# Accumulator banks of the third chunk pair, order of evacuations, and place of the first parted hidden chunks in a two-layer transformer kernel

## The chip, the cores and the metric

The kernel runs on one core of a Trainium2 chip. The metric is the device time of one execution in microseconds; the time before is the median of 3 runs. The engines are TensorE (PE, with its weight loads PEld), VectorE (DVE), ScalarE (ACT), GpSimd (POOL) and SyncE (SP, which here issues the loads of the weights).

## The reference

Two layers (DEPTH = 2), a sequence of 512 tokens, model width 1024, hidden width 2816. In each layer two feed-forward stages stand around a mix of three attention branches:

```python
def _swiglu(x, w1, w2):
    gt, up = jnp.split(x @ w1, 2, axis=-1)
    return (jax.nn.silu(gt) * up) @ w2

for l in range(DEPTH):
    x = _layer_norm(DN_ALPHA * x + 0.5 * _swiglu(x, ffn1_w1[l], ffn1_w2[l]), ln1_g[l], ln1_b[l])
    mix = _token_mix(x, w_in[l], ...)
    x = _layer_norm(DN_ALPHA * x + mix, ln2_g[l], ln2_b[l])
    x = _layer_norm(DN_ALPHA * x + 0.5 * _swiglu(x, ffn2_w1[l], ffn2_w2[l]), ln3_g[l], ln3_b[l])
```

The change lies in the feed-forward stages, of which there are four: FFN1 and FFN2 of layer 0, FFN1 and FFN2 of layer 1.

## The kernel before

**Parts.** Every fp32 operand is held as a high part and a low part (`hi`/`lo` for weights, `xh`/`xl` for the activations), and a product is three matmuls: hi·hi, hi·lo, lo·hi. ACT makes a high part by a rounding copy, DVE the low part by a subtraction (L159 and L160 in `wsplit`). The parts of weights lie in rotating buffers of several pools; `unit()` deals them out in a fixed cycle. In the feed-forward stage the cycle over seven units is: shared pool `wt` (3 buffers), `more` twice, `w1` twice, `wt` twice.

**Stages of a feed-forward block** (`ffn`). The hidden width is cut into 22 chunks of 128. For chunk `f` a gate and an up column block are multiplied with the activations, and `evac` writes Silu(gate)·up to the hidden buffer (L380 on ACT, then L381 on DVE).

1. Chunks 0 and 1 are done in `staged`: four accumulators `pj` (gate 0, up 0, gate 1, up 1), all with the first 256 tokens, then all with the second 256. Their weights were prepared during the stage before. Between the first products the transposes of the last token blocks of the normalised activations run (`second`, L238; L240 and L241 take them out of PSUM), two banks for token block 2 and two for token block 3.
2. Chunk 2 is a plain pair, `pg` and `pu`, each 24 matmuls of 512 columns (L180 to L182).
3. Chunks 3 to 21 compute gate and up together with seven half-size products in place of eight (`seven` prepares the weights, `seven_products` multiplies). `seven` loads two raw blocks through SP (L304, L306), splits the gate block (`ug`, L159 and L160), forms two sums and differences on DVE (`x1`, `x2`, L312 to L315), parts them (`u1`, `u2`, L317 and L318) and parts half of the up block (`ud`: `dh`, `dl`, L319 and L320). The order of the products is `ug`, `u1`, `u1`, `u2`, `ud`, `ug`, `u2`: 12 half-size matmuls each (L334), 84 in a chunk. They use three accumulators, `pg`, `pu`, `pv`. The activations' side needs sums over tokens (`token_sums`, L362 to L367), made once for each stage; `lth` is their last ACT and last DVE instruction.
4. `rows_ln` multiplies the hidden chunks with the rows of the second weight matrix into eight accumulators `acc` (L193 to L195) and applies the layer norm. A hidden chunk is parted before (`h_parts`, L386 and L387); chunks 0 and 1 are parted into one `hi` and one `lo` buffer of the shared pool `wt`, before the loop's last chunk is prepared (L417 to L420), the others into buffers of their own.

**PSUM banks.** There are eight, under four tags: `mm` 2, `sc` 3, `tp` 2, `po` 1. `ps()` without a tag deals them out in a ring: the counter `ring[0]` picks the tag, and each tag rotates its own buffers. Four accumulators `pj` and four transposes make eight, so the ninth and tenth allocations, `pg` and `pu` of chunk 2, come back to the ring places of the first `pj` pair.

**Order.** PE and POOL follow the order in which the program is written. ACT, DVE and SP are ordered by a scheduler when the program is built; `behind(a, b)` tells it to issue what follows no earlier than instructions a and b. Before the change, chunks 3, 4 and 5 and the evacuations of chunks 0, 1 and 2 are all behind `lth`. In the order built from that, ACT takes after chunk 3's first split the Silu table load, the two Silus of chunks 0 and 1 and chunk 4's split, and then both L317 of chunk 3; DVE does the two L381 and chunk 4's L160 before chunk 3's L318. At the end, ACT and DVE part hidden chunks 0 and 1 before they split chunk 21's weights.

Of the kernel before, what the change touches and what calls it, by code (L numbers as in the profile page):

```python
# [10 lines left out]
F32 = mybir.dt.float32  # L11
F32R = mybir.dt.float32r
BF = mybir.dt.bfloat16
AF = mybir.ActivationFunctionType
OP = mybir.AluOpType
# [4 lines left out]
P = 128  # L20
S, D, F = 512, 1024, 2816
KD, KF, NB = D // P, F // P, S // P
# [43 lines left out]
def body(tc, a, out, depth=DEPTH):  # L66
    nc = tc.nc
# [7 lines left out]
    wt = pool("wt")  # L75
# [4 lines left out]
    ring = [0]  # L80
# [50 lines left out]
    lnq = K()  # L131
    lnq.sq = None

    def behind(*ins):

        st = ExitStack()
        for i in ins:
            if i:
                st.enter_context(tc.issue_after(i))
        return st  # L140
# [150 lines left out]
    PLAIN = (0, 1, 2)  # L291
# [6 lines left out]
    def seven(w, ca, cb, pl, ru):  # L298

        v = w.rearrange("(k p) f -> p k f", p=P)
        rg = wraw()
        nc.sync.dma_start(rg, v[:, :, ca:ca + P])  # L304
        ru = ru or wraw()
        nc.sync.dma_start(ru, v[:, :, cb:cb + P])  # L306
        ug, u1, u2 = wsplit(rg), unit(), unit()
        ud = [pl.tile([P, 4, P], F32R, name=n, tag=n) for n in ("dh", "dl")]
        h1, h2 = slice(0, 4), slice(4, 8)
        x1, x2 = [pl.tile([P, KD, P], F32, name="ws", tag="ws", bufs=2) for _ in range(2)]  # L310
        tt = nc.vector.tensor_tensor
        tt(x1[:, h1], ru[:, h1], ru[:, h2], op=OP.add)  # L312
        tt(x1[:, h2], x1[:, h1], rg[:, h1], op=OP.subtract)
        tt(x2[:, h1], rg[:, h1], ru[:, h1], op=OP.subtract)
        tt(x2[:, h2], rg[:, h2], x1[:, h2], op=OP.subtract)  # L315
        for (hi, lo), x in ((u1, x1), (u2, x2)):
            nc.scalar.activation(hi, x, AF.Copy)  # L317
            tt(lo, x, hi.bitcast(F32), op=OP.subtract)  # L318
        nc.scalar.activation(ud[0], ru[:, h2], AF.Copy)  # L319
        tt(ud[1], ru[:, h2], ud[0].bitcast(F32), op=OP.subtract)  # L320
        return ug, u1, u2, ud

    def seven_products(ws, t, pl, u, nb):

        (ug, u1, u2, ud), (t1, t2, t3, t4) = ws, t
        ga, pa, pb = ps(name="pg"), ps(name="pu"), ps(name="pv")
        p_, r_, s_ = [(xh[:, k:k + 4, c], xl[:, k:k + 4, c]) for k, c in ((0, H1), (4, H1), (4, H2))]

        def prod(o, w, k0, x, first=True):
            for k in range(4):  # L330
                hi, lo = w[0][:, k0 + k], w[1][:, k0 + k]
                vh, vl = x[0][:, k], x[1][:, k]
                for i, (wx, vx) in enumerate(((hi, vh), (hi, vl), (lo, vh))):
                    nc.tensor.matmul(o, wx, vx, start=first and k == 0 and i == 0, stop=k == 3 and i == 2,  # L334
                                     skip_group_check=True)

        tt = nc.vector.tensor_tensor
        prod(ga[:, H1], ug, 0, p_)
        prod(ga[:, H2], u1, 0, t1, False)
        sn = pl.tile([P, S], F32, name="sn", tag="sn", bufs=nb)  # L340
        nc.scalar.activation(sn, ga, AF.Copy)  # L341
        prod(pa[:, H1], u1, 4, t2)
        prod(pa[:, H2], u2, 0, t3, False)
        v = pl.tile([P, S], F32, name="v", tag="v", bufs=nb)
        tt(v[:, H1], pa[:, H1], sn[:, H1], op=OP.add)
        tt(v[:, H2], pa[:, H2], v[:, H1], op=OP.add)
        prod(pb[:, H1], ud, 0, t4)
        tt(u[:, H1], pb[:, H1], v[:, H2], op=OP.add)
        tt(u[:, H2], sn[:, H2], v[:, H2], op=OP.add)
        prod(ga[:, H1], ug, 4, r_, False)  # L350
        prod(ga[:, H2], u2, 4, s_, False)
        tt(ga[:, H2], ga[:, H2], v[:, H1], op=OP.add)
        return ga
# [15 lines left out]
    def ffn(l, w1, w2, which, xap, xa, wts, pend, done_prev, last, nxt, late=None):  # L369


        st = K()
        NA = KF - NTAIL

        def hpart(f):
            return (st.ha, st.hb)[f >= NA][:, f - NA * (f >= NA)]

        def evac(f, pg, pu):
            t = st.lnp.tile([P, S], F32, name="t", tag="t", bufs=2)
            nc.scalar.activation(t, pg, AF.Silu)  # L380
            nc.vector.tensor_tensor(hpart(f), t, pu, op=OP.mult)  # L381

        hs = {}

        def h_parts(k, t):
            nc.scalar.activation(t[:, 0], hpart(k), AF.Copy)  # L386
            nc.vector.tensor_tensor(t[:, 1], hpart(k), t[:, 0].bitcast(F32), op=OP.subtract)  # L387
            hs[k] = t

        pts = staged(wts, pend)  # L390
        for tb in range(NB):
            nc.gpsimd.dma_start(x_sp[tb * P:(tb + 1) * P, :], xa[tb])
        done_prev()
        xap.release()
        st.w1p = nx.w1 = pool("w1p", side="right", reuse_waits="tile")
        more.n = 4
        with behind(lnq.sq):
            wp = [(wcols(w1, f * P), wcols(w1, F + f * P)) for f in PLAIN[2:]]

        for n, shape, dt, nb in (("hi", [P, KD, P], F32R, 2), ("lo", [P, KD, P], F32R, 2), ("dh", [P, 4, P], F32R, 1),  # L400
                                 ("dl", [P, 4, P], F32R, 1), ("raw", [P, KD, P], F32, 1), ("sn", [P, S], F32, 2),
                                 ("v", [P, S], F32, 2), ("ws", [P, KD, P], F32, 2)):
            st.w1p.tile(shape, dt, name=n, tag=n, bufs=nb)
        th, tl = (st.w1p.tile([P, 4, 4, 256], F32R, name=n) for n in ("th", "tl"))
        tpl, nb = (pre_t, 6) if late else (st.w1p, 2)
        lth = [token_sums(k, lambda: tpl.tile([P, KD, P], F32, name="ws", tag="ws", bufs=nb)
                          .rearrange("p a s -> p (a s)"), th, tl) for k in range(4)][-1]
        st.t = [(th[:, i], tl[:, i]) for i in range(4)]
        if late:
            late()  # L410
        fb = pool("fb", reuse_waits="tile")
        st.lnp = pool("lnp", reuse_waits="tile")
        fa = pool("fa", reuse_waits="tile")
        st.hb = fb.tile([P, NTAIL, S], F32, name="hb")
        st.ha = fa.tile([P, NA, S], F32, name="ha")
        for f in range(2, KF):
            if f == KF - 1:  # L417
                for k, n in enumerate(("hi", "lo")):
                    h_parts(k, wt.tile([P, KD, P], F32R, name=n, tag=n, bufs=3)
                            .rearrange("p (a b) c -> p a (b c)", a=2))  # L420
            if f not in PLAIN:
                ru = nx.w1.tile([P, KD, P], F32, name="raw", tag="raw") if f % 2 else None
                with behind(*(lth if f < 6 else ())):
                    ws = seven(w1, f * P, F + f * P, nx.w1, ru)
                    if f == PLAIN[-1] + 1:
                        evac(0, pts[0], pts[1])
                        evac(1, pts[2], pts[3])
                        for x in wp:
                            evac(*x)
                evac(f, seven_products(ws, st.t, nx.w1, hpart(f), 2), hpart(f))  # L430
                continue
            wg, wu = wp.pop(0)
            pg, pu = ps(name="pg"), ps(name="pu")
            proj(pg, wg)
            proj(pu, wu)
            wp.append((f, pg, pu))
        nx.w1 = None
        st.w1p.tile([P, 88], F32, name="pad")
        st.w1p.release()
        xap, xa = alloc_xa()  # L440
        for tb in range(NB):
            nc.gpsimd.dma_start(xa[tb], x_sp[tb * P:(tb + 1) * P, :])
        hsp = pool("hsp", side="right", reuse_waits="tile")
        ln = LN(hsp, which, l, xa, 0.5, last)

        def wload(k):
            if k not in hs:
                h_parts(k, hsp.tile([P, 2, S], F32R, name="hs", tag="hs", bufs=6))
            w = wrows(w2, k)
            if after and k > 2:  # L450
                i, h = after.pop(0)
                nc.gpsimd.tensor_copy(pace, w[1][:, 0, 0:1].bitcast(F32))
                nc.gpsimd.dma_start(bvec[i, h:h + 1], bsml[i, h:h + 1, None, :].to_broadcast([1, P, TLEN]))
            return w

        wts, pend = rows_ln(KF, wload, lambda k: hs[k][:, 0], lambda k: hs[k][:, 1], ln, NA, fa.release, nxt)

        def done():
            nx_close()
            hsp.release()  # L460
            st.lnp.release()
            fb.release()

        return wts, pend, done, xap, xa
# [983 lines left out]
```

## Time and profile before

| | |
|---|---|
| Median of 3 runs | 2504.3 us (2503.48 to 2506.77) |
| The profiled execution, own time | 2505.77 us |
| Its span | 2504.0 us |
| Mean granted TensorE clock | 0.993 |
| DMA | 286.29 MB, mean 114 GB/s |
| ACT L159 waits for raw weight loads, total | 62.7 us in 26 waits |
| Loads of feed-forward weights | 264, 512 KB each, 3.9 us to landing |

A row of a timeline has start, duration, engine, line, operation, output and inputs, and in brackets the idle time of the engine before it with what ended it. A row of the waits has who waited for whom, the total, the number of times and the longest. A row of windows has the busy time of each engine in a stretch of the span, then the granted clock and the DMA share. The chunk numbers in the text are the loop index `f`. Chunk 2 begins at 41.0 us (FFN1, layer 0), 927.3 (FFN2, layer 0), 1281.2 (FFN1, layer 1) and 2166.4 (FFN2, layer 1).

### The profile page before, as it was taken

What the parts mean: (1) busy time and instruction counts of PE and PEld (TensorE: products, weight loads), DVE (VectorE), ACT (ScalarE), POOL (GpSimd) and SP (SyncE); (2) the same over time, 40 slices, a digit from 0 to 9 for tenths busy, and PEclk for the clock granted to TensorE, in tenths of its full rate; (3) what the DMA queues carried; (4) which work ended last, traced back from release to release, by engine and by line L of the source; (5) the groups of instructions that cost most, each with busy time, mean ns of one, the idle gap of its engine ahead of it and who ended that gap; (6) DMA issues with size and microseconds to landing.
All of it is one profiled execution on the core that took longest, in us unless ns stands there. A gap on an engine that the chain in (4) does not pass through costs nothing.

```text
span 2504.0 us, 42423 instructions
## 1 busy us (share of the span) xinstructions
PE 2465.6 (98%) x16411; PEld 2213.7 (88%) x16411; DVE 1795.1 (72%) x3661; ACT 1173.1 (47%) x2208; POOL 228.7 (9%) x454
## 2 busy tenths in 40 slices
PE   9999999999999989999999999999999999899998
PEld 8999887788889889998899998878888998899986
DVE  7997355587688688974499963566777886888734
ACT  4544334477644444543344443345666444444431
POOL 2000210133300000000000000002332000000000
PEclk9999999999999999999999999999999999999999
DMA  6333543633134433334334343445322344333341
GB/s 189 114 106 100 194 118 119 179 81 93 44 101 136 140 102 97 109 93 160 101 105 115 102 145 109 133 116 149 101 74 68 93 135 135 95 108 102 109 144 59
DMA packets 378106, 286.29 MB, mean 114 GB/s; under 512 B 17464, under 2 KB 349384, under 8 KB 377904
## 3 DMA queue, kind: packets, MB, share of 16 engines
q1 hardware_dynamic: 370496, 258.68, 35.1%
q0 software_dynamic: 7408, 24.90, 2.8%
q8 instruction: 129, 2.11, 0.3%
q14 instruction: 73, 0.60, 0.1%
HBM read 256.22 MB, written 17.88 MB: 109 GB/s over the span
## 4 chain that ended last, share of the span: by engine, by line
PE 93%; DVE 4%; DMA 1%; ACT 1%; issue 1%; SPq 0%; DVEq 0%; POOLq 0%; ACTq 0%; POOL 0%
PE pg L334 21%; PE pu L334 10%; PE acc L194 8%; PE acc L193 8%; PE acc L195 8%; PE pv L334 5%; PE pj L180 5%; PE pj L181 4%; PE pj L182 4%; PE brp L180 2%; PE brp L181 2%; PE brp L182 2%; PE sN L913 2%; PE ptN L955 1%; PE po L974 1%; PE sF L834 1%
## 5 line engine op out<-in xcount | busy, mean ns | idle before, releaser
L160 DVE TENSOR_TENSOR lo<-raw,hi 128x1024 fp32r<-128x1024 f32 (+1 forms) x314 | 375.9, 1203 | 310.4 <-ACT hi L159 303.9
L159 ACT ACTIVATE hi<-raw 128x1024 fp32r<-128x1024 f32 (+1 forms) x314 | 324.4, 1040 | 416.0 <-PE acc L194 195.8
L334 PE MATMUL pg<-xh,hi 128*128 128x256 f32 x1104 | 312.4, 283 | 0.2 <-ACT sn L341 0.2
L334 PE MATMUL pg<-xh,lo 128*128 128x256 f32 x1104 | 312.4, 283 | 0.0
L334 PE MATMUL pg<-xl,hi 128*128 128x256 f32 x1104 | 312.4, 283 | 0.0
L317 ACT ACTIVATE hi<-ws 128x1024 fp32r<-128x1024 f32 x184 | 193.8, 1058 | 169.5 <-DVE ws L315 47.3
L180 PE MATMUL pj<-xh,hi 128*128 128x512 f32 (+1 forms) x720 | 267.6, 372 | 0.6 <-ACT hi L159 0.6
L318 DVE TENSOR_TENSOR lo<-ws,hi 128x1024 fp32r<-128x1024 f32 x184 | 224.1, 1221 | 57.7 <-ACT hi L317 57.4
L182 PE MATMUL pj<-xh,lo 128*128 128x512 f32 (+1 forms) x720 | 255.2, 354 | 0.0
L181 PE MATMUL pj<-xl,hi 128*128 128x512 f32 (+1 forms) x720 | 254.9, 354 | 0.1
L193 PE MATMUL acc<-hi,hs 128*128 128x512 f32 x640 | 249.5, 390 | 0.0
L195 PE MATMUL acc<-lo,hs 128*128 128x512 f32 x640 | 249.1, 389 | 0.0
L194 PE MATMUL acc<-hi,hs 128*128 128x512 f32 x640 | 249.0, 389 | 0.0
L334 PEld LDWEIGHTS pg<-xh,hi 128*128 128x128 f32 x1104 | 211.9, 192 | 1.2 <-ACT sn L341 0.4
L334 PEld LDWEIGHTS pg<-xl,hi 128*128 128x128 f32 x1104 | 211.9, 192 | 0.8
L334 PEld LDWEIGHTS pg<-xh,lo 128*128 128x128 f32 x1104 | 211.9, 192 | 0.0
L334 PE MATMUL pu<-th,hi 128*128 128x256 f32 x608 | 172.9, 284 | 4.4 <-ACT hi L317 4.4
L334 PE MATMUL pu<-th,lo 128*128 128x256 f32 x608 | 173.0, 285 | 3.0 <-DVE lo L318 3.0
L334 PE MATMUL pu<-tl,hi 128*128 128x256 f32 x608 | 172.5, 284 | 0.0
L182 PEld LDWEIGHTS pj<-xh,lo 128*128 128x128 f32 x720 | 136.8, 190 | 19.7 <-DVE lo L160 0.2
L180 PEld LDWEIGHTS pj<-xh,hi 128*128 128x128 f32 x720 | 137.1, 190 | 16.4 <-issue 3.7
L181 PEld LDWEIGHTS pj<-xl,hi 128*128 128x128 f32 x720 | 137.5, 191 | 11.6 <-DVE xl L1389 0.3
(341 smaller groups left out, 5945.2 us busy)
## 6 DMA issues: line engine op xcount, KB each, us to landing
raw<-in_ffn_w_dram SPq DMA_DIRECT2D x264, 512.0 KB, 3.9
raw<-in_w_in_dram SPq DMA_DIRECT2D x56, 512.0 KB, 3.8
raw<-in_w_gate_dram SPq DMA_DIRECT2D x48, 512.0 KB, 3.9
x_sp<-xa POOLq DMA_DIRECT2D x24, 512.0 KB, 5.8
ks<-hl SPq DMA_DIRECT2D x96, 128.0 KB, 2.4
xa<-x_sp POOLq DMA_DIRECT2D x16, 512.0 KB, 6.2
raw<-in_w_out_dram SPq DMA_DIRECT2D x16, 512.0 KB, 3.5
tab<-bvec SPq DMA_DIRECT2D x16, 256.0 KB, 4.1
```

What stands on the lines that cost most here:

```text
L159: nc.scalar.activation(hi[:, c], raw[:, c], AF.Copy)
L160: nc.vector.tensor_tensor(lo[:, c], raw[:, c], hi[:, c].bitcast(F32), op=OP.subtract)
L180: nc.tensor.matmul(o, hi[:, k], vh, start=first, stop=False)
L181: nc.tensor.matmul(o, hi[:, k], vl, start=False, stop=False)
L182: nc.tensor.matmul(o, lo[:, k], vh, start=False, stop=last)
L193: nc.tensor.matmul(o, sh(k)[:, t], hi[:, c], start=k == 0, stop=False)
L194: nc.tensor.matmul(o, sl(k)[:, t], hi[:, c], start=False, stop=False)
L195: nc.tensor.matmul(o, sh(k)[:, t], lo[:, c], start=False, stop=k == nk - 1)
L317: nc.scalar.activation(hi, x, AF.Copy)
L318: tt(lo, x, hi.bitcast(F32), op=OP.subtract)
L334: nc.tensor.matmul(o, wx, vx, start=first and k == 0 and i == 0, stop=k == 3 and i == 2, skip_group_check=True)
L913: nc.tensor.matmul(o[:, 0:nb].rearrange("p k b j -> p (k b j)"), q, kx[:, 2 * b0:2 * (b0 + nb)].rearrange("p a b -> p (a b)"), start=i == ...
```

## The change

It has four pieces, all in `ffn` but the first.

- `seven` records its last ACT and DVE instructions of parting `u1` and `u2` (L317, L318) in `lnq.parted`.
- Ahead of the chunk loop the ring counter is moved on by four places. The pair of chunk 2 then takes the ring places of token block 2's two transposes, and everything dealt out of the ring later is shifted by four places.
- Chunk 3's weights stay behind `lth`; chunks 4 and 5 are now behind the parting of the chunk before; the evacuations of chunks 0, 1 and 2 are behind the parting of chunk 3.
- Hidden chunks 0 and 1 are parted after `seven` of the last chunk has been written out, in place of before it.

```diff
         for (hi, lo), x in ((u1, x1), (u2, x2)):
-            nc.scalar.activation(hi, x, AF.Copy)
-            tt(lo, x, hi.bitcast(F32), op=OP.subtract)
+            pa = nc.scalar.activation(hi, x, AF.Copy)
+            pv = tt(lo, x, hi.bitcast(F32), op=OP.subtract)
+        lnq.parted = (pa.ins, pv.ins)
...
+        ring[0] += 4
         for f in range(2, KF):
-            if f == KF - 1:
-                for k, n in enumerate(("hi", "lo")):
-                    h_parts(k, wt.tile([P, KD, P], F32R, name=n, tag=n, bufs=3)
-                            .rearrange("p (a b) c -> p a (b c)", a=2))
             if f not in PLAIN:
                 ru = nx.w1.tile([P, KD, P], F32, name="raw", tag="raw") if f % 2 else None
-                with behind(*(lth if f < 6 else ())):
+                with behind(*(lth if f == PLAIN[-1] + 1 else lnq.parted if f < 6 else ())):
                     ws = seven(w1, f * P, F + f * P, nx.w1, ru)
+                with behind(*lnq.parted):
                     if f == PLAIN[-1] + 1:
                         evac(0, pts[0], pts[1])
                         evac(1, pts[2], pts[3])
                         for x in wp:
                             evac(*x)
+                if f == KF - 1:
+                    for k, n in enumerate(("hi", "lo")):
+                        h_parts(k, wt.tile([P, KD, P], F32R, name=n, tag=n, bufs=3)
+                                .rearrange("p (a b) c -> p a (b c)", a=2))
                 evac(f, seven_products(ws, st.t, nx.w1, hpart(f), 2), hpart(f))
```

## The prediction, made before the changed kernel ran

> **What bounds the kernel now.** I read the page's busy lines and chain first, then TensorE's own waits, then the timeline around each wait.
>
> ```profile
> span 2504.0 us, 42423 instructions
> PE 2465.6 (98%) x16411; PEld 2213.7 (88%) x16411; DVE 1795.1 (72%) x3661; ACT 1173.1 (47%) x2208; POOL 228.7 (9%) x454
> PE 93%; DVE 4%; DMA 1%; ACT 1%; issue 1%; SPq 0%; DVEq 0%; POOLq 0%; ACTq 0%; POOL 0%
> ```
>
> TensorE (PE) is busy for 98% of the span and makes up 93% of the chain of waits. Its instruction list is the same in both built programs, so the change can only win where PE stands still or runs at a low clock. Those places, from the waits of PE alone (total us, times, longest us):
>
> ```profile
> PE pg L180 <- ACT t L380: 13.1, 2, 6.6
> PE pu L334 <- ACT hi L317: 4.4, 4, 1.1
> PE pu L334 <- DVE lo L318: 3.0, 4, 0.8
> ```
>
> All three belong to feed-forward stages. The first is two long waits, one in each second feed-forward stage (FFN2). The others are a pair of short waits in each of the four stages.
>
> **Edit 1: the third pair takes other banks.** The PE timeline at chunk 2 in the FFN2 of layer 1, then of layer 0 (start us, duration us):
>
> ```profile
> 2159.62 0.28 PE L182 MATMUL pj<-xh,lo 128*128 128x256 f32 x1
> 2166.36 0.80 PE L180 MATMUL pg<-xh,hi 128*128 128x512 f32 x1 [6.46 <-ACT t L380]
> ...
> 2174.63 0.39 PE L180 MATMUL pu<-xh,hi 128*128 128x512 f32 x1
> ...
> 2180.07 0.28 PE L334 MATMUL pg<-xh,hi 128*128 128x256 f32 x1
> ...
> 920.42 0.28 PE L182 MATMUL pj<-xh,lo 128*128 128x256 f32 x1
> 927.29 0.80 PE L180 MATMUL pg<-xh,hi 128*128 128x512 f32 x1 [6.59 <-ACT t L380]
> ...
> 941.02 0.28 PE L334 MATMUL pg<-xh,hi 128*128 128x256 f32 x1
> ```
>
> Chunk 2's `pg` lands in the bank of the first pair's gate and waits until its Silu (L380) has read it. The second half, 24 matmuls from 2174.63 to 2180.07, takes 5.44 us, 0.227 each. The first half takes 8.27, 2.83 more, because after the wait the clock is low:
>
> ```profile
> 2160.00:2185.00 25.00, 18.64 (x90) 16.01 (x91) 21.00 (x29) 12.59 (x15) 0.00 (x0) 0.80 0.30 85
> ```
>
> This window has a granted clock of 0.80 (after the busy times of PE, PEld, DVE, ACT, POOL). Undisturbed, last `pj` matmul to chunk 3 is 0.12 + 48 x 0.227 = 11.00. Measured: 20.45 (layer 1) and 20.60 (layer 0). Excess 9.45 + 9.60 = **19.05 us**.
>
> The counter moved by 4 gives the pair the two banks of the first of the two late transposes; the buffer addresses in the built program say so. Who reads those banks, and what the engines do at that time:
>
> ```profile
> 2139.75 2.35 DVE L160 TENSOR_TENSOR lo<-raw,hi 128x1024 fp32r<-128x1024 f32 x2
> 2142.02 1.28 DVE L241 TENSOR_TENSOR xl<-pt,xh 128x512 fp32r<-128x512 f32 x2
> 2145.74 1.29 DVE L241 TENSOR_TENSOR xl<-pt,xh 128x512 fp32r<-128x512 f32 x2 [2.44 <-ACT xh L240]
> 2164.11 0.68 DVE L312 TENSOR_TENSOR ws<-raw 128x512 f32<-128x512 f32 x1
> 2164.41 1.28 ACT L380 ACT_TABLE_LOAD   x1
> 2164.71 1.22 DVE L160 TENSOR_TENSOR lo<-raw,hi 128x1024 fp32r<-128x1024 f32 x1
> 2165.71 1.08 ACT L380 ACTIVATE t<-pj 128x512 f32<-128x512 f32 x2
> 2167.05 0.68 DVE L313 TENSOR_TENSOR ws<-ws,raw 128x512 f32<-128x512 f32 x1
> 2170.58 2.43 DVE L318 TENSOR_TENSOR lo<-ws,hi 128x1024 fp32r<-128x1024 f32 x2
> ```
>
> The transposes' banks are read out by 2143.3 and 2147.0, well before 2159.7, and chunk 2's weights are split by 2142.1 (the first row). So chunk 2 follows the staged half at once and ends at 2159.62 + 11.00 = 2170.62. What is late next is chunk 3's weights, which now have 9.4 us less.
>
> **Edit 2: evacuations behind chunk 3's weights, chunk 4 and 5 behind the chunk before.** On ACT the table load and the first two Silus move behind both L317 of chunk 3; on DVE the first two L381 and chunk 4's first split move behind both L318. Six DVE instructions (L312, L160, L314, L320, L313, L315) then run from 2164.11 at the spacing of the rows (0.60, L160 at most 1.22), to 2168.3. ACT starts `u1` hi when L313 is done, near 2167.8, and takes 1.06 (the L317 row below): 2168.8. `u1` lo ends at about 2170.0, `u2` lo at 2171.2 (1.2 each, half of the 2.43 row). Chunk 3 from 2170.62 has 12 matmuls of 0.12 on `ug` first, so `u1` is due at 2172.06 and `u2` at 2174.94. Slack 2.0 and 3.7. Even at the old times (`u2` lo done at 2173.0) the second would fit.
>
> Queued behind on ACT: table load 1.28 from 2169.9, then the two Silus, done at about 2172.2. Their reader is chunk 3's `pv`, which takes the first pair's gate bank 48 half matmuls (5.76 us) into the chunk, at 2176.4; slack 4.7. Chunk 4 takes the next three banks at 2180.7; the DVE reaches the two L381 at about 2172 to 2173.
>
> For chunk 4 the DVE's load must be known. Ten undisturbed chunks of 10.08 us:
>
> ```profile
> 69.45:170.25 100.80, 100.80 (x842) 100.80 (x842) 92.60 (x148) 48.25 (x62) 0.00 (x0) 1.00 0.37 106
> ```
>
> DVE (third busy figure) works 9.26 us a chunk, 0.82 is free. From 2164.11 to `u2`'s due time of chunk 4, 2180.7 + 4.32 = 2185.0, are 20.9 us; two whole chunks of DVE work and the first pairs' two L381 (0.60 each, the size of L312) are 19.7, and this counts sums that come later. So I price edit 2 at **0**; its cover is at least 1.2 us of DVE time, and what exceeds it reaches PE one for one. The pairs of weight loads on SP change only their order among themselves (gate, up, gate, up instead of gate, gate, up, up) and are issued before their data is due; price 0, bounded by the rival below.
>
> Edits 1 and 2 also touch the first stages (FFN1):
>
> ```profile
> 41.00 0.50 PE L180 MATMUL pg<-xh,hi 128*128 128x512 f32 x1 [0.31 <-DVE init L1366]
> 52.01 0.28 PE L334 MATMUL pg<-xh,hi 128*128 128x256 f32 x1
> 1281.18 0.40 PE L180 MATMUL pg<-xh,hi 128*128 128x512 f32 x1
> 1292.46 0.28 PE L334 MATMUL pg<-xh,hi 128*128 128x256 f32 x1
> ```
>
> Against 10.88 for 48 matmuls they take 11.01 (plus the 0.31 wait) and 11.28: 0.44 + 0.40 = **0.8 us** to gain. In layer 0 the new banks were last used by the tables, and chunk 3's `u1` lo, due 1.44 us into the chunk and done at 53.41 (the row below), moves ahead of two evacuations and one split.
>
> ```profile
> 52.20 1.21 DVE L318 TENSOR_TENSOR lo<-ws,hi 128x1024 fp32r<-128x1024 f32 x1
> ```
>
> **Edit 3: hidden chunks 0 and 1 parted behind the last weights.** PE, ACT and DVE in the last stage, then whole windows from chunk 20's second part to chunk 21's in all four stages, and one undisturbed chunk (width, PE busy, granted clock, DMA share, GB/s):
>
> ```profile
> 2365.96 1.06 ACT L317 ACTIVATE hi<-ws 128x1024 fp32r<-128x1024 f32 x1 [0.78 <-PE pu L334]
> 2367.05 1.23 DVE L318 TENSOR_TENSOR lo<-ws,hi 128x1024 fp32r<-128x1024 f32 x1 [3.56 <-ACT hi L317]
> 2367.07 0.39 PE L334 MATMUL pu<-th,hi 128*128 128x256 f32 x1 [1.09 <-ACT hi L317]
> 2368.33 0.39 PE L334 MATMUL pu<-th,lo 128*128 128x256 f32 x1 [0.76 <-DVE lo L318]
> ...
> 230.73:244.63 13.90, 12.06 (x86) 0.88 0.00 1
> 1119.73:1132.18 12.45, 10.60 (x87) 1.00 0.00 0
> 1471.67:1484.11 12.44, 10.60 (x86) 1.00 0.00 1
> 2358.79:2371.23 12.44, 10.59 (x86) 1.00 0.00 1
> 220.65:230.73 10.08, 10.08 (x86) 1.00 0.50 158
> ```
>
> The parted chunks take a `hi` and a `lo` buffer of the shared pool before chunk 21's weights do, so chunk 21's `u2` gets the buffer of its own `u1`: ACT cannot write it until PE has used `u1`, and PE needs `u2` next. Excess over 10.08: 3.82 + 2.37 + 2.36 + 2.36 = **10.91 us**. In the changed program the three have buffers of their own, and the parts take `u1`'s, free 4.32 us into chunk 21. Each part is one L386 and one L387 (mean ns of one behind the busy time):
>
> ```profile
> L387 DVE TENSOR_TENSOR hs<-ha,hs 128x512 fp32r<-128x512 f32 x64 | 42.2, 685 | 5.6 <-ACT hs L386 5.6
> L386 ACT ACTIVATE hs<-ha 128x512 fp32r<-128x512 f32 x64 | 37.5, 617 | 7.9 <-PE acc L195 7.9
> ```
>
> Both parts then end about 6.3 us in (4.32 + 2 x 0.62 + 0.69); the output product needs them at 10.08. Below nothing there is no gain to add; if instead the buffer came free only at the chunk's end, one L386 and one L387 would stand before PE, 1.3 to 1.4 a stage, 5.6 in all at most. I take 0, since the addresses show the early buffer.
>
> The 1.85 us waits left the clock at 1.00 three times and at 0.88 once; the 6.5 us waits halved it. [...]
>
> **Sum:** 19.05 + 10.91 + 0.8 = 30.8 us. The profiled execution took 2505.77 (span 2504.0 and 1.8 around it), 1.5 above the median 2504.3: 2475.0 for it, **2473.5** for the median. I say 2474.
>
> **The rivals.**
> *A weight wait takes the place of the removed one.* For: PE comes 9.4 us earlier on a DVE that stood at 21.0 of 25 us busy there. Against: the slacks above. If half the excess came back in both FFN2: 2474 + 9.5 = 2483. It begins when DVE or a load slips by more than 2 us.
>
> *Edit 3 does nothing*, because chunk 21 still finds a shared buffer. Against: the addresses. Time 2474 + 10.9 = 2485.
>
> *Slower: the new order makes DVE idle inside every chunk.* Parting chunks 4 and 5 reshuffles all later chunks on ACT and DVE, whose queues run in order. If the order costs DVE 1.32 us a chunk in waits on PE, PE loses 0.5 in each of 4 x 19 chunks, 38 us: 2512. Beyond 0.82 + 30.8/76 = 1.23 it eats the whole gain. For: the share of 92%. Against: the built order still has a later chunk's weight work ahead of each sum that waits on PE, so DVE has something to do until PE is there.
>
> **How the numbers follow.** Forecast 0.74, weight wait 0.11, edit 3 without effect 0.05, slower 0.07, gains and losses that cancel 0.03. About 0.2% (5 us) is what a measurement tells from no change. Faster 0.90, same 0.03, slower 0.07. The forecast's own range is 2471 (spread of the runs shown, 1 to 2 us) to 2481 (5.6 and the clock term of 1.5 above). With the two partial cases it reaches 2486; the slower case is left out.
>
> **What would show it.** Edit 1: no wait of PE at L180 on L380, and about 11.0 us from the last staged matmul to chunk 3 in both FFN2. Edit 2: no PE wait on L317 or L318 in chunks 3 to 5, and DVE still near 92% in the chunks after. Edit 3: the four windows at 10.08, and no wait at the first output product. Wrong would be: new PE waits on weights in chunk 3 or 4 (first rival), windows still at 12.4 (second), small PE waits repeated in every chunk (third).

## The result, and the profile after

| | before | changed |
|---|---|---|
| Median | 2505.53 us (2503.48 to 2507.45, 4 runs) | 2475.08 us (2473.36 to 2476.26, 4 runs) |
| Ratio, 95% interval | | 0.9878 (0.9861 to 0.9895) |
| Profiled execution, its span | 2505.77, 2504.0 | 2473.36, 2471.6 |
| Granted clock | 0.993 | 0.999 |

The changed kernel is 30.45 us faster by the medians (that of the kernel before has one run more than the one given above). The head of its page, and the engines' shares of its chain of waits:

```profile
span 2471.6 us, 42378 instructions
...
PE 2454.2 (99%) x16411; PEld 2206.7 (89%) x16411; DVE 1786.7 (72%) x3661; ACT 1161.8 (47%) x2208; POOL 228.1 (9%) x454
...
PE 97%; DVE 1%; DMA 1%; SPq 0%; issue 0%; ACT 0%; DVEq 0%; POOLq 0%; POOL 0%; ACTq 0%
```

TensorE has the same 16411 matmuls, yet is busy 11.4 us less (2465.6 before): most of that part of the gain, about 8.6, is matmuls that no longer run at a granted clock of 0.50 (1.5 in the staged half of the first stage, 1.5 at its chunk 21, 2.8 behind each of the two long waits). The rest of the 32.4 us between the two spans is idle time of TensorE. The waits of PE that are left (total us, times, longest us):

```profile
PE xT L1390 <- DMA xa<-in_x_dram: 4.3, 1, 4.3
PE ptS L807 <- ACT p L548: 0.9, 2, 0.5
PE cum L636 <- DVE p L546: 0.9, 2, 0.6
PE pj L180 <- ACT hi L159: 0.5, 1, 0.5
```

The three feed-forward rows of before are gone: no wait on L380 (now L381), none on L317 or L318. The long row that remains is the first load of x.

Chunk 2 and the start of chunk 3 in the FFN2 of layer 1, from the timeline of the changed kernel (start, duration, engine, line; `evac`'s Silu is now L381, its product L382, the seven products L335):

```profile
2139.00 0.28 PE L182 MATMUL pj<-xh,lo 128*128 128x256 f32 x1
2139.12 0.40 PE L180 MATMUL pg<-xh,hi 128*128 128x512 f32 x1
...
2147.15 2.01 ACT L317 ACTIVATE hi<-ws 128x1024 fp32r<-128x1024 f32 x2 [3.35 <-DVE ws L313]
...
2148.24 2.36 DVE L318 TENSOR_TENSOR lo<-ws,hi 128x1024 fp32r<-128x1024 f32 x2 [0.41 <-ACT hi L317]
...
2149.18 1.28 ACT L381 ACT_TABLE_LOAD   x1
...
2150.03 0.28 PE L335 MATMUL pg<-xh,hi 128*128 128x256 f32 x1
...
2150.47 1.09 ACT L381 ACTIVATE t<-pj 128x512 f32<-128x512 f32 x2
...
2151.13 1.28 DVE L382 TENSOR_TENSOR ha<-t,pj 128x512 f32<-128x512 f32 x2
...
2151.70 0.28 PE L335 MATMUL pg<-th,lo 128*128 128x256 f32 x1
```

Chunk 2 follows the last staged matmul at once, and chunk 3 starts 11.03 us after that matmul (20.45 before). Chunk 3's `u1` lo, the first of the two L318, is done near 2149.4; the first product that reads it is the row at 2151.70, so 2.3 us are to spare. The Silus and their products come behind, and nobody on PE waits for them.

Chunk 21 in the four stages, over the same stretch of work as the windows shown of before, then ten undisturbed chunks (width, then busy time of PE, PEld, DVE, ACT, POOL; granted clock, DMA share, GB/s):

```profile
229.04:239.12 10.08, 10.08 (x86) 10.08 (x86) 4.31 (x9) 2.98 (x5) 0.00 (x0) 1.00 0.01 2
1104.81:1114.89 10.08, 10.08 (x86) 10.08 (x86) 4.31 (x9) 2.95 (x5) 0.00 (x0) 1.00 0.00 0
1453.51:1463.59 10.08, 10.08 (x86) 10.08 (x86) 4.31 (x9) 2.95 (x5) 0.00 (x0) 1.00 0.00 0
2328.74:2338.82 10.08, 10.08 (x87) 10.08 (x86) 4.31 (x9) 2.95 (x5) 0.00 (x0) 1.00 0.01 2
67.80:168.60 100.80, 100.80 (x842) 100.80 (x841) 92.16 (x145) 48.74 (x63) 0.00 (x0) 1.00 0.39 111
```

All four stretches have the regular 10.08 (13.90 and three times 12.4 before). DVE still works 9.2 us in each chunk of 10.08, and PE has no gap there.

**Where the time went, matmul by matmul.** Both programs issue the same matmuls in the same order, so each one's start in before minus its start in the changed kernel shows where the changed kernel's lead grows (from the two profiled executions):

| Place | Lead gained, us | Term of the sum |
|---|---|---|
| staged half, FFN1 layer 0 (from 32.2 us of before) | 1.49 | none |
| chunk 2, FFN1 layer 0 | 0.34 | 0.44 |
| chunk 21, FFN1 layer 0 | 3.82 | 3.82 |
| chunk 2, FFN2 layer 0 | 9.57 | 9.60 |
| chunk 21, FFN2 layer 0 | 2.37 | 2.37 |
| chunk 2, FFN1 layer 1 | 0.37 | 0.40 |
| after chunk 3, FFN1 layer 1 (from 1300.05 us of before) | 0.49 | none |
| chunk 21, FFN1 layer 1 | 2.37 | 2.36 |
| chunk 2, FFN2 layer 1 | 9.43 | 9.45 |
| chunk 21, FFN2 layer 1 | 2.36 | 2.36 |

With 0.2 lost in other places these are the 32.4 us. The two rows without a term are not the change's. The first lies ahead of everything that the change touches: it is a stretch of 3.41 us from 32.0 us at a granted clock of 0.50, which run 1 below has as well, though it has the new banks, and run 3 has not, though chunk 2 is as before there. The second is gained by runs 3 and 5 as well, which leave chunks 2 to 20 as they were. Without them the changed program gains 30.6.

### The profile page after: what moved, and what is told of

It reads as the page before. It is cut to its first block, busy times and chain, and to the rows that moved or that the text cites. A ratio compares the mean times of both kernels' runs of the same rounds, so it can differ in the third digit from the quotient of the medians.

```text
span 2471.6 us, 42378 instructions
## 1 busy us (share of the span) xinstructions
PE 2454.2 (99%) x16411; PEld 2206.7 (89%) x16411; DVE 1786.7 (72%) x3661; ACT 1161.8 (47%) x2208; POOL 228.1 (9%) x454
## 4 chain that ended last, share of the span: by engine, by line
PE 97%; DVE 1%; DMA 1%; SPq 0%; issue 0%; ACT 0%; DVEq 0%; POOLq 0%; POOL 0%; ACTq 0%
PE pg L335 21%; PE pu L335 11%; PE acc L195 8%; PE acc L194 8%; PE acc L193 8%; PE pv L335 5%; PE pj L180 5%; PE pj L182 5%; PE pj L181 5%; PE brp L180 2%; PE brp L181 2%; PE brp L182 2%; PE sN L917 2%; PE ptN L959 1%; PE po L978 1%; PE po L865 1%
## 5 line engine op out<-in xcount | busy, mean ns | idle before, releaser
L335 PE MATMUL pg<-xh,lo 128*128 128x256 f32 x1104 | 312.4, 283 | 0.0
L335 PE MATMUL pg<-xl,hi 128*128 128x256 f32 x1104 | 312.4, 283 | 0.0
L335 PE MATMUL pg<-xh,hi 128*128 128x256 f32 x1104 | 312.3, 283 | 0.0
L317 ACT ACTIVATE hi<-ws 128x1024 fp32r<-128x1024 f32 x184 | 191.9, 1055 | 127.3 <-DVE ws L313 63.4
L318 DVE TENSOR_TENSOR lo<-ws,hi 128x1024 fp32r<-128x1024 f32 x184 | 223.2, 1220 | 37.7 <-ACT hi L317 37.3
L335 PEld LDWEIGHTS pg<-xh,hi 128*128 128x128 f32 x1104 | 211.9, 192 | 0.8
L335 PEld LDWEIGHTS pg<-xl,hi 128*128 128x128 f32 x1104 | 211.9, 192 | 0.8
L335 PEld LDWEIGHTS pg<-xh,lo 128*128 128x128 f32 x1104 | 211.9, 192 | 0.0
L335 PE MATMUL pu<-th,hi 128*128 128x256 f32 x608 | 172.1, 283 | 0.0
L335 PE MATMUL pu<-tl,hi 128*128 128x256 f32 x608 | 172.1, 283 | 0.0
L335 PE MATMUL pu<-th,lo 128*128 128x256 f32 x608 | 172.1, 283 | 0.0
L181 PEld LDWEIGHTS pj<-xl,hi 128*128 128x128 f32 x720 | 136.9, 190 | 11.6 <-DVE xl L1393 0.3
```

Source lines behind the costliest of these rows:

```text
L181: nc.tensor.matmul(o, hi[:, k], vl, start=False, stop=False)
L317: pa = nc.scalar.activation(hi, x, AF.Copy)
L318: pv = tt(lo, x, hi.bitcast(F32), op=OP.subtract)
```

## The experiments

The first four ran beside the kernel before at 2503.26 us (2502.72 to 2507.55, 7 runs), the other four beside it at 2504.55 (2502.51 to 2507.52, 11 runs). These two medians and the 2505.53 beside the changed kernel are all of the kernel before, so a comparison between runs that stand beside different ones can be off by up to 2.3 us. The theory is that of the prediction: edits 1 and 3 each remove a wait of their own, and edit 2 is only cover for edit 1.

**1. The banks alone (edit 1).**

```diff
         st.ha = fa.tile([P, NA, S], F32, name="ha")
+        ring[0] += 4
         for f in range(2, KF):
```

> Only the ring counter is moved on by four; order and parted chunks as before. Theory (the bank alone makes chunk 2 wait): both 6.5 us waits of PE on L380 in FFN2 and the low clock behind them go, the 19.05 us; with 0.8 from FFN1, 2505.5 - 19.9 = 2485.6. In the old order chunk 3's u1 lo ends 0.5 us before it is due, so no wait on L317 or L318 in chunk 3. Rival (the evacuations' order is needed too): PE waits on chunk 3's weights in both FFN2, 2 us or more each, 2490 or above. The 10.9 us at chunk 21 stay in both.

Measured: 2484.08 us (2483.86 to 2485.26), ratio 0.9919 (0.9905 to 0.9934), 19.2 faster. Of the three waits that the prediction starts from, these are left:

```profile
PE pu L334 <- ACT hi L317: 4.4, 4, 1.1
...
PE pu L334 <- DVE lo L318: 3.0, 4, 0.8
```

They are the pairs at chunk 21, unchanged. Moving the pair to other banks is what takes the 6.5 us waits away, and chunk 3's weights come in time even in the old order, but for 0.2 us in the FFN1 of layer 0 (run 4 shows the rows).

**2. The order alone (edit 2): evacuations and the weights of chunks 4 and 5 behind the parted weights, old banks, old place of the hidden chunks.**

```diff
+        lnq.parted = (pa.ins, pv.ins)
...
-                with behind(*(lth if f < 6 else ())):
+                with behind(*(lth if f == PLAIN[-1] + 1 else lnq.parted if f < 6 else ())):
                     ws = seven(w1, f * P, F + f * P, nx.w1, ru)
+                with behind(*lnq.parted):
                     if f == PLAIN[-1] + 1:
```

> Only the order: evacuations behind chunk 3's weights, chunks 4 and 5 behind the chunk before; banks and parted chunks as before. Theory (the bank binds, and the moved Silus come later): the first Silu ends near 2171.7 in the last FFN2 in place of 2166.3, so PE waits 11.9 us there in place of 6.5, and chunk 2's up product in FFN1 waits 5 to 7 us on the second Silu: about 2 x 5.4 + 7.3 + 5.5 = 24 us more, with up to 6 of low clock, 2529 to 2535. Rival (the order itself gains or is neutral): 2505 or below.

Measured: 2533.49 us (2533.19 to 2534.25), ratio 1.0116 (1.0101 to 1.0131), 30.2 slower. Its first two waits of PE, and the place of the wait in the FFN2 of layer 1:

```profile
PE pg L180 <- ACT t L381: 23.7, 2, 11.8
PE pu L180 <- ACT t L381: 12.6, 2, 7.2
```

```profile
2189.85 2.36 DVE L318 TENSOR_TENSOR lo<-ws,hi 128x1024 fp32r<-128x1024 f32 x2 [0.40 <-ACT hi L317]
...
2192.08 1.08 ACT L381 ACTIVATE t<-pj 128x512 f32<-128x512 f32 x2
...
2192.73 0.79 PE L180 MATMUL pg<-xh,hi 128*128 128x512 f32 x1 [11.84 <-ACT t L381]
```

With the old banks the Silu that reads the first pair's gate is what PE waits for. Edit 2 puts it behind chunk 3's parting, and the 6.5 us wait becomes 11.8; the first stages, which hardly waited, now wait 5 to 7 us too. So edit 2 by itself is a loss, and it is free only where chunk 2 no longer needs the first pair's banks.

**3. The hidden chunks alone (edit 3).** Only the four lines that part hidden chunks 0 and 1 move behind `seven` of chunk 21, as in the change.

> Only hidden chunks 0 and 1 are parted behind the last weights. Theory: the pair of waits on L317 and L318 goes from all four chunks 21, windows of 10.08, 4 x 2.36 = 9.4 us, and 1.5 more in runs where the clock had dropped in one of them: 2505.5 - 9.4 to 10.9 = 2494.6 to 2496.1. Rival (the wait moves to the parts, or to the first output product): nothing gained, 2504 to 2506. The long waits in FFN2 stay.

Measured: 2492.76 us (2492.24 to 2493.48), ratio 0.9953 (0.9938 to 0.9968), 10.5 faster. Of the three waits that the prediction starts from this one is left:

```profile
PE pg L180 <- ACT t L380: 12.9, 2, 6.5
```

**4. Edits 1 and 3, without 2.** The edits of runs 1 and 3 together.

> Banks and parted chunks as in the changed kernel, the order as before. Theory (edit 2 was priced at 0): as the changed kernel, 2475.1 within 1.5, no PE wait on L317 or L318 in chunk 3. Rival (edit 2 gives chunk 3 its weights in time): 2 us or more above the changed kernel in each FFN2, 2479 or above, with those waits in the trace.

Measured: 2475.14 us (2473.45 to 2476.59), ratio 0.9885 (0.9868 to 0.9901): the time of the full change. The gains of runs 1 and 3 add up to 29.7 (19.2 and 10.5); this run gains 28.1 and the full change 30.5 over the medians beside them, so the parts add up within what the medians move. Edit 2 moves no time that the medians can show. Chunk 3 of this run shows why this is closer than it looks, first in the FFN2 of layer 1, then in the FFN1 of layer 0:

```profile
2150.08 1.22 DVE L318 TENSOR_TENSOR lo<-ws,hi 128x1024 fp32r<-128x1024 f32 x1
...
2151.82 0.28 PE L334 MATMUL pg<-th,lo 128*128 128x256 f32 x1
...
50.99 1.21 DVE L318 TENSOR_TENSOR lo<-ws,hi 128x1024 fp32r<-128x1024 f32 x1
...
52.25 0.39 PE L334 MATMUL pg<-th,lo 128*128 128x256 f32 x1
```

In the FFN2 of layer 1 `u1` lo ends at 2151.30 and is read at 2151.82: 0.5 us to spare in place of 2.3. In the FFN1 of layer 0 it ends at 52.20 and its reader starts at 52.25, 0.24 behind the matmul before it in place of 0.12. Matmul by matmul this run and run 1 lose 0.22 us there, which edit 2 saves: all that it is worth as things stand.

**5. Why chunk 21 waited.** The kernel before, with the hidden chunks still parted first, but the unit counter moved on by two for chunk 21's weights, so that its three parted weights take three buffers.

```diff
+                    if f == KF - 1:
+                        more.n += 2
                     ws = seven(w1, f * P, F + f * P, nx.w1, ru)
+                    if f == KF - 1:
+                        more.n -= 2
```

> The kernel before, whose hidden chunks 0 and 1 are still parted ahead of chunk 21's weights; only the counter of weight units is moved by 2 for chunk 21, so that its three weights take three different buffers and none waits for its own u1. Theory (the shared buffer is what made PE wait at chunk 21): the pair of waits at L317 and L318 is gone in all four stages, chunk 21 lasts 10.08 us, and the gain is that of edit 3 alone (10.5 us, of which 9.4 to 10.9 were predicted): 2503.3 - 10.5 = 2492.8 (2492.0 to 2494.5). Rival (the parting work on ACT and DVE ahead of the weights is what came late): the waits stay or shift, 2501 to 2505.

Measured: 2493.00 us (2491.26 to 2494.70), ratio 0.9953 (0.9938 to 0.9967), 11.6 faster, as much as moving the parts. The waits on L317 and L318 are gone; the long ones are still there:

```profile
PE pg L180 <- ACT t L380: 13.0, 2, 6.5
```

The parting work ahead of the weights costs nothing; the shared buffer was the cause.

**6. How much cover edit 2 gives.** The changed kernel with DVE held up ahead of chunk 3's weights: the last low part of the token sums is written four times.

```diff
+        hi_ = nc.scalar.activation(th[:, :, k], t, AF.Copy).ins
+        for _ in range(again):
+            tt(tl[:, :, k], t, th[:, :, k].bitcast(F32), op=OP.subtract)
+        return hi_, tt(tl[:, :, k], t, th[:, :, k].bitcast(F32), op=OP.subtract).ins
...
-                          .rearrange("p a s -> p (a s)"), th, tl) for k in range(4)][-1]
+                          .rearrange("p a s -> p (a s)"), th, tl, 3 * (k == 3)) for k in range(4)][-1]
```

> The changed kernel; the last low part of the token sums (L367), which stands on DVE ahead of chunk 3's weights in every stage, is written four times instead of once, so that DVE reaches these weights about 3.4 to 3.7 us later (three more of 1.14 to 1.22 us). Theory (edit 2 makes u1 lo ready about 2 us before it is due): 1.1 to 1.7 us lost in each of four stages, 4.5 to 7 us: 2475.1 + 5.5 = 2480.6 (2479 to 2483), with a PE wait on u1 lo at chunk 3. Rival (the slack is far larger than I worked out): no change, 2475. Rival (edit 2's order gives no slack at all): 4 x 3.5 = 14 us or more lost, 2489 or above, the same as the next run.

Measured: 2483.75 us (2481.91 to 2485.45), ratio 0.9916 (0.9901 to 0.9930): 8.7 above the changed kernel. The waits, then chunk 3 in the last stage (L317 and L318 keep their lines, the products are at L335):

```profile
PE pg L335 <- DVE lo L318: 3.0, 4, 0.8
PE pg L335 <- ACT hi L317: 2.4, 4, 1.1
```

```profile
2152.27 3.75 DVE L369 TENSOR_TENSOR tl<-ws,th 128x1024 fp32r<-128x1024 f32 x3 [1.13 <-ACT th L367]
2156.05 1.23 DVE L370 TENSOR_TENSOR tl<-ws,th 128x1024 fp32r<-128x1024 f32 x1
...
2161.97 0.39 PE L335 MATMUL pg<-th,hi 128*128 128x256 f32 x1 [0.42 <-ACT hi L317]
...
2163.22 0.39 PE L335 MATMUL pg<-th,lo 128*128 128x256 f32 x1 [0.75 <-DVE lo L318]
```

The three added operations hold DVE up by 3.78 us (2152.27 to 2156.05). Matmul by matmul the loss against the changed kernel is 1.70 in each of three stages, so 2.1 of the 3.78 were covered, near the 2.3 read off above. In the FFN1 of layer 0 the loss is 3.79: the waits are 1.09 and 0.76 there, and the granted clock is 0.50 from 57.00 to 60.41 us. The four make 8.9 where 5.5 were expected (at most 7): the 1.70 is the upper end of what was worked out for a stage, and the other 2.1 come in the first stage alone. The time lies 0.75 above the expected range.

**7. The same delay without edit 2.** Edits 1 and 3, with the three added operations.

> Edits 1 and 3 without edit 2 (2475.1 us by itself), with the same three added low parts on DVE. Theory (the old order leaves u1 lo at best just in time, since the evacuations' two or three L381 and chunk 4's first split stand ahead of it): the whole delay of 3.4 to 3.7 us reaches PE in each stage, 14 us: 2489 (2485 to 2495 with what the clock loses in the longer waits). The difference to the run before, near 9 us, is what edit 2's order covers. Rival (the order is worth nothing even then): the same time as the run before.

Measured: 2497.52 us (2495.25 to 2497.98), ratio 0.9968 (0.9955 to 0.9980): 22.4 above the same kernel without the delay, and 13.8 above run 6.

```profile
PE pg L334 <- ACT hi L317: 11.6, 4, 3.3
...
PE pg L334 <- DVE lo L318: 2.7, 4, 0.8
```

The delay passes through nearly whole: 14.3 us of waits, 3.6 a stage of 3.78. The expected 14 us were the waits alone; each stage loses 5.5 (6.4 in the first), because the clock drops behind every one of these waits (to 0.50 from 1295.13 to 1298.55 us in the FFN1 of layer 1, for example). The time is 2.5 above the top of the expected range, which allowed too little for that. So edit 2 is worth next to nothing today and 13.8 us against a DVE that is 3.8 us late.

**8. Other wrong banks.** The kernel before with the counter moved by two, so that chunk 2 takes the banks of later staged products.

```diff
+        ring[0] += 2
```

> The kernel before with the counter of banks moved by 2 instead of 4: the third pair then takes banks of the last pj products, which are read out by the second and third Silu of the evacuations (L380, L381), not by the transposes' readers. Theory (what decides is which work reads the bank out): PE still waits for L380 or L381 in both FFN2, about 1 to 3 us longer than before, and in FFN1 too: 2505 to 2520. Rival (any move away from the first pair's bank gives most of edit 1's gain): 2484 to 2488, as with edit 1 alone.

Measured: 2513.16 us (2512.12 to 2515.63), ratio 1.0034 (1.0023 to 1.0046), 8.6 slower. Its first wait of PE, and its place in the last stage:

```profile
PE pg L180 <- ACT t L380: 19.8, 3, 7.2
```

```profile
2171.60 1.09 ACT L380 ACTIVATE t<-pj 128x512 f32<-128x512 f32 x2
...
2172.74 0.79 PE L180 MATMUL pg<-xh,hi 128*128 128x512 f32 x1 [7.00 <-ACT t L380]
```

The two long waits stay, 0.5 us longer each, and a third of 5.6 appears in the FFN1 of layer 0. That was expected in both FFN1, and came in one only. Matmul by matmul that stage loses 7.4 us; the two FFN2 even gain 0.6 and 0.8, because the clock of 0.50 behind the long wait lasts twice 3.41 us there and three times (10.24 us) in the kernel before (runs 3 and 5, with the old banks, have two in the last stage as well, so there it need not be the edit's doing); and the clock drops twice more behind chunk 21's waits, 1.5 us each (to 0.50 from 1134.70 to 1138.11 us in the FFN2 of layer 0). Not any other bank helps: of the two other places tried, only the one that the transposes' readers empty early does.

## Why the prediction was right

*Edit 1.* Each step held: the wait on the Silu is gone, chunk 2 to chunk 3 takes 11.03 in both FFN2 (11.00 worked out), and the excess of 9.45 and 9.60 became a gain of 9.43 and 9.57. That the banks do it is shown by run 1, and by run 8 that it is their reader that counts. The 2.83 us of low clock behind the wait (granted 0.50 from 2161.93 to 2172.17 us in the last stage of before) were rightly part of the price.

*Edit 2, priced at nothing.* Run 4 confirms the zero: 2475.14 without it against 2475.08 with it, and 0.22 us by the matmuls. The cover that the prediction named, at least 1.2 us of DVE time and a slack of 2.0 for `u1`, was 2.3 by the rows and 2.1 by run 6. The prediction had what exceeds it reach PE one for one. By the rows 1.5 of the 3.78 exceeded it; PE lost 1.70 in three stages, and 3.79 in the one where the clock dropped as well, so that holds, roughly, only where the clock stays. What the prediction did not say is that the old order would nearly have fitted too, with 0.5 us to spare in the last stage and 0.2 short in the first.

*Edit 3.* All four stretches are 10.08, and the gain by the table above is 10.9 (10.91 predicted). The named cause, one buffer shared by `u1` and `u2`, is shown by run 5, which removes the sharing, leaves the parts where they were, and gains the same 10.9 in the four chunks 21, as run 3 does. The parts end as forecast: hidden chunk 1's last operation starts at 2337.13, takes 0.69, and chunk 21, which began at 2331.46, ends at 2341.54.

```profile
2335.86 0.63 ACT L387 ACTIVATE hi<-ha 128x512 fp32r<-128x512 f32 x1 [0.72 <-PE pu L335]
...
2337.13 0.69 DVE L388 TENSOR_TENSOR lo<-ha,lo 128x512 fp32r<-128x512 f32 x1
...
2341.54 0.40 PE L193 MATMUL acc<-hi 128*128 128x512 f32 x1
```

The clock drop in the first stage (granted 0.50 from 240.23 to 243.64 us of before) is what makes its term 3.82 where the others are 2.36 and 2.37, and the table has 3.82 there. The medians alone could not tell whether it belongs in the sum: 30.45 us were gained, 30.8 is the sum with it and 29.3 without it, and the medians of the kernel before differ by 2.3.

*The first stages.* 0.8 was priced, 0.34 and 0.37 came, from edit 1: run 1 has both, run 3 neither.

*The rivals.* The weight wait does not occur, since no wait on L317 or L318 is left; the delay that it needs is the 2.1 us of run 6. The second rival fails with the four windows. For the slower one DVE would have had to lose 1.23 us in every chunk: its busy time is 9.2 of 10.08 as before and PE has no gap in ten chunks.

*What the sum left out.* It took before's profiled execution as all due to the program. Of its 2504.0 us, 1.49 in the staged half and 0.49 near 1300 us were not the program's to lose: other kernels with the same code there are without them. The term 3.82 of edit 3 holds 1.5 us (3.82 less 2.37, the clock term of the forecast's range) of a clock drop that came in one stage of four, and which stages have it differs from one profiled execution to the next (below). That the sum, with this drop in it, came within 0.4 us of the medians is in part luck; none of these is larger than the spread of the runs.

## What to carry to other kernels

When PE waits for an accumulator bank, ask who reads that bank last and when: moving the allocation to a bank that had been read out 16 us before it was needed (2143.3 and 2159.7 in the last stage of before) took two waits away, while a move by half as many places made things slower. A new order of the side engines that saves next to nothing on top of such a gain, and without it cost 30 us, may be what keeps the gain from resting on half a microsecond, and a deliberate delay ahead of the covered work measures that cover directly. Before a short wait is put down to an engine, check which buffers its operands share: two runs with quite different edits gained the same time here, because both gave these operands buffers of their own.

## What the runs showed of the hardware that was not expected

A short wait of PE cost clock as well in some places of these runs and not in others. In the kernel before the granted clock falls from 1.00 to 0.50 at 32.01, 240.23, 922.89, 2161.93 and 2496.44 us. From one of these times to the next are 61, 200, 363 and 98 times 3.413 us, and the clock is back at 1.00 after one such width in the first two and after three (10.24 us) in the next two; the last stays low to the end of the program. The windows below are cut at whole widths from these times, and in another run from the times of its own drops. Those around chunk 21's pair of waits in the kernel before, with the window behind them, first in the FFN1 of layer 0, then in the FFN2 of layer 0 (columns as above, the clock third from the end):

```profile
236.81:240.23 3.42, 1.62 (x12) 1.21 (x10) 1.22 (x1) 1.37 (x2) 0.00 (x0) 1.00 0.00 0
240.23:243.64 3.41, 3.37 (x15) 3.37 (x16) 0.79 (x2) 0.00 (x0) 0.00 (x0) 0.50 0.02 5
...
1124.28:1127.69 3.41, 2.65 (x23) 2.45 (x21) 0.16 (x1) 1.38 (x2) 0.00 (x0) 1.00 0.00 0
1127.69:1131.11 3.42, 2.33 (x17) 2.13 (x18) 1.56 (x2) 0.28 (x1) 0.00 (x0) 1.00 0.00 0
1131.11:1134.52 3.41, 3.41 (x30) 3.41 (x30) 1.37 (x4) 0.98 (x1) 2.11 (x4) 1.00 0.24 70
```

The same waits of 1.09 and 0.76 us fall into one window in the first case (PE busy 1.62 of 3.42) and the next window has a clock of 0.50; in the second they are split over two windows (2.65 and 2.33 busy) and the clock stays at 1.00. Over the pairs of waits at chunk 21 in this kernel and runs 1, 2 and 8, and those at chunk 3 in runs 6 and 7, 24 in all, the clock dropped behind 12. Idle time is counted here as in these rows, the width less PE's busy time. In the 12 without a drop no window held more than 1.44 us of it (1479.27 to 1482.68 us in the kernel before, PE busy 1.97 of 3.41); in the 12 with one, the window ahead of it held 1.65 or more. The two in which the idle times come closest, from run 2 (chunk 21, FFN2 of layer 1) and run 7 (chunk 3, FFN1 of layer 1):

```profile
2392.13:2395.54 3.41, 1.76 (x12) 1.56 (x13) 1.23 (x1) 0.84 (x1) 0.00 (x0) 1.00 0.00 0
2395.54:2398.96 3.42, 3.42 (x18) 3.42 (x17) 1.70 (x4) 0.00 (x0) 0.51 (x1) 0.50 0.00 0
...
1288.31:1291.72 3.41, 1.71 (x14) 1.46 (x12) 3.41 (x6) 0.65 (x2) 0.00 (x0) 1.00 0.00 0
1291.72:1295.13 3.41, 1.60 (x11) 1.39 (x12) 3.41 (x5) 2.06 (x2) 0.00 (x0) 1.00 0.78 218
```

1.65 us idle were followed by a clock of 0.50 in the first. In the second 1.70 were followed by 1.00 (1.63 in the last stage of run 7 as well), and the drop came only behind the 1.81 of the next window. Nothing closer can be read off these records, the ends of matmuls being modelled. A drop behind chunk 21's pair cost 1.5 us each time. This is read off the records of the runs above, and no kernel was made to move a wait along the windows; that it also explains part of the 5 us spread of the kernel before is a guess, and was not tried.

One drop does not follow idle time at all by this measure, the one in the staged half of the kernel before:

```profile
28.59:32.00 3.41, 3.41 (x32) 3.41 (x32) 3.41 (x9) 1.60 (x2) 0.00 (x0) 1.00 0.55 192
32.00:35.42 3.42, 3.42 (x19) 3.42 (x18) 0.94 (x2) 2.95 (x4) 0.00 (x0) 0.50 0.85 240
```

PE is busy throughout the window ahead of it, most of the time with 27 matmuls of 32 columns (28.21 to 31.39 us). Five of the ten profiled executions have this drop (the kernel before, runs 1, 5, 6 and 7) and five have not. Why is open.
